# A hybrid gMLP and dilated-attention layer on one core: heads in one pipeline, gating inside the attention, last values through the rows' buffers

## The chip, the cores and the metric

The kernel runs on one core of a Trainium2 chip. A core has TensorE (PE in the profile, its weight loads PEld), VectorE (DVE), ScalarE (ACT), GpSimd (POOL) and SyncE (SP), whose queue issues nearly all DMAs here. The metric is the device time of one execution in microseconds. The kernel before took 1597.32 us, the median of 3 runs (1597.07 to 1600.4).

## The reference

One layer over 1024 tokens of width 1024, in float32:

```python
h = rms_norm(x, g_pre); proj = h @ w_in          # u, v, z_A, q, k, v_B, z_B, gate_A, gate_B
y_a = u' * (W_s LN(v') + b) * silu(z_a)           # gMLP: 16 groups, mixing inside 128-token chunks
for (window, dilation) in ((128,1),(512,4),(2048,16)):
    s = q.k * E**-0.5 - slope*dist                # 8 heads of 128, ALiBi, |j| <= 64 steps
    o, lse = softmax(s) @ v, logsumexp(s)
y_b = sum(softmax(lse over patterns) * o) * silu(z_b)
m = sigmoid(gate_a)*(y_a @ w_pa) + sigmoid(gate_b)*(y_b @ w_pb)
out = x + rms_norm(m @ w_o, g_post)
```

## The kernel before

Every float32 product is made as three products of rounded parts: an operand is split into a high part (ACT copies it into a rounded type) and a low part (the rest, a subtraction on DVE or POOL), and PE adds high by high, high by low and low by high. So each product needs an ACT and a DVE or POOL instruction ahead of PE.

The stages, in order of time:
- **Rows and attention values.** Tiles of x are normalised and transposed; `vb` is the product with the value columns of `w_in`, made in banks for several chunks at once. `v_out` (line 249) splits a bank into `vh` and `vl` and stores both to DRAM. `vh` has two buffers of the tag "ws", `vl` two of its own. The last call of `rows_product` ends with four such banks.
- **Projections.** All other columns of `w_in` go through a seven-product scheme (`seven`, line 369). The first column block is `gates(0)`: its products are called `g0p`. Its second product, `p6`, needs a sum of two weight blocks (`weight_sum`, line 364 in `sum_of`), and that sum's tile has the tag "ws" too. Then come the gMLP columns with the mixing.
- **Attention beside the A projection.** For each head: `scores` (eight pairs of 128-query tiles; half 1 is the residue classes, half 0 the chunks, of which 0 and 7 are the end chunks with narrower windows), the exponentials on ACT, `exchange` of maxima and sums between the two layouts (16 small copies on POOL, 16 on DVE), `normalise`, `scale` of the weights, and `weigh`: nine stages (four residues, chunks 1 and 3, the ends, chunks 5 and 7), each transposing weights on PE (line 723), splitting the transposed bank (`pth`, `ptl`), and multiplying with the values (`pr` line 742, `pc` line 757) two stages later (`LAG`). The sum of both is `o`, stored to `o_d` (line 804). The products of the A projection (`pa`, lines 857 to 859) are cut into 256 steps of three products; `BESIDE` says how many go with each stage, `PAIRS` how many score pairs of the next head. After its ninth stage a head takes its last two stages' products at once, and then the next head begins.
- **Tail.** `gated_heads` loads `o_d` and the gate `z_d` for two heads and half the tokens at a time, multiplies them on POOL (line 925) and splits the result into `yh`, `yl`; the steps that are left run beside it. Then PE makes `pb` (lines 977 to 979), and last the output projection with the final norm.

The order of instructions on each engine is set when the program is built, by a list scheduler over the code's order; the engines then run their own lists in order and wait on semaphores. Buffers of one tag are reused in rotation: who takes one waits until its last reader, a store included, is done.

Of the kernel before, what the change touches and what calls it, by code (L numbers as in the profile page):

```python
# [9 lines left out]
F32 = mybir.dt.float32  # L10
# [26 lines left out]
def tile_hybrid_encoder(  # L37
# [164 lines left out]
    with tc.tile_pool(name="start", bufs=1) as sp:  # L202
# [46 lines left out]
        def v_out(c, cb, ps):  # L249
            vh = wpool.tile([P, 512], F32R, tag="ws", bufs=2, name=f"vh{cb}{c}")  # L250
            vl = sp.tile([P, 512], F32R, tag="vl", bufs=2, name=f"vl{cb}{c}")
            split(vh, vl, ps)
            for t, d in ((vh, v_hi), (vl, v_lo)):
                stored.append(nc.sync.dma_start(d[c * P:(c + 1) * P, 512 * cb:512 * (cb + 1)], f32(t)))
# [321 lines left out]
    with tc.tile_pool(name="heads", bufs=1) as hp, tc.tile_pool(name="attn", bufs=1) as ap:  # L576
# [45 lines left out]
        def scores(h, res):  # L622
# [6 lines left out]
            order = [(1, (i, i + 1)) for i in (0, 2, 4, 6)] + [(0, (0, 7)), (0, (1, 2)), (0, (3, 4)), (0, (5, 6))]  # L629
            for half, pair in order:  # L630
                ps = bank("sc", f"sc{h}{half}{pair[0]}").rearrange("p (t n) -> p t n", t=2)
                st = (hp if half else ap).tile([P, 2, 256], F32, tag=f"st{half}", bufs=8 if half else 6, name=f"st{h}{half}{pair[0]}")
# [79 lines left out]
        def weigh(h, res):  # L712

# [83 lines left out]
            for stage in begun:  # L797
                take(stage)

            for b in range(2):  # L800
                hs = slice(512 * b, 512 * (b + 1))
                o4 = o[:, hs].rearrange("p (a i r) -> p a i r", a=4, r=4)
                nc.vector.tensor_tensor(o4, po[b].rearrange("p (a r i) -> p a i r", a=4, r=4), o4, ALU.add)
                nc.sync.dma_start(o_d[h][:, hs], o[:, hs])

# [14 lines left out]
        PAIRS = (2, 2, 2, 2, 0, 0, 0, 0, 0)  # L820
        BESIDE = (2, 1, 1, 2, 1, 2, 3, 3, 3, 4)
# [62 lines left out]
        for _ in queries_keys(1, heads[1]):  # L884
            take(steps, 3)
        for h in range(H):
# [3 lines left out]
            for i, _ in enumerate(weigh(h, heads[h])):  # L890
                take(pairs, PAIRS[i])
                take(steps, BESIDE[i])
                if i == 3 and more:
                    residue_values(h + 1, heads[h + 1])
                if more and i == 3:
                    take(exchange(h + 1, heads[h + 1], 0))
                    late = exchange(h + 1, heads[h + 1], 1)
                if more and i in (5, 6):
                    take(late, 1)
                if more and i == 7:  # L900
                    normalise(h + 1, heads[h + 1])
                if more and i == 8:
                    for tile_ in TILES[0] + TILES[1]:
                        scale(heads[h + 1], *tile_)
                if i > 4:
                    take(ahead, 1)
            if more:
                chunk_values(h + 1, heads[h + 1])
            take(ahead)
            take(steps, BESIDE[9])  # L910


    with tc.tile_pool(name="tail", bufs=1) as tp:
# [3 lines left out]
        def gated_heads(h, b):  # L917

            bs = slice(512 * b, 512 * (b + 1))
            o, z = [tp.tile([P, 2, 512], F32, tag=t, bufs=n, name=f"{t}{h}{b}") for t, n in (("o", 2), ("z", 1))]  # L920
# [8 lines left out]
        ready = (_ for h in range(0, H, 2) for b in range(2) for _ in gated_heads(h, b))  # L929
# [133 lines left out]
```

## Time and profile before

| what | value |
|---|---|
| median of 3 runs | 1597.32 us |
| the profiled execution, its span | 1596.76 us, 1595.0 us |
| PE busy | 1519.5 us, 95% |
| DVE, POOL, ACT busy | 55%, 48%, 43% |
| mean granted clock of PE | 0.982 |
| DMA | 252.16 MB, 158 GB/s over the span |

PE is busy nearly throughout, so time is to be found where PE stands or runs at the lower clock. A busy matmul is counted from its start to its modelled end and overlaps the next one; the pace of PE is seen in the distance between starts.

### The profile page before, as it was taken

The page shows a single profiled execution, that of the slowest core. Times are in us where ns is not written, and L with a number is a line of the kernel's source. Part 1 is how long each engine was busy: PE and PEld are TensorE (multiplying, and loading weights), DVE is VectorE, ACT ScalarE, POOL GpSimd, SP SyncE. Part 2 cuts the span into 40 slices and gives each one's busy share as a digit, 9 for nine tenths or more (in the row PEclk, how much of TensorE's full clock was granted, in tenths as well). Part 3 has the DMA queues.
Part 4 walks back from the last instruction along what each step waited for, and adds up shares of the span by engine and source line. Part 5 has one row for each costly group of instructions (what it writes and reads, how often), then busy time and mean ns, then how long its engine had stood idle before and what let it go on. Part 6 is the DMA issues. An engine that isn't in the chain of part 4 may idle for free. (4 is left out here: it accounts for less than half of the span.)

```text
span 1595.0 us, 22762 instructions
## 1 busy us (share of the span) xinstructions
PE 1519.5 (95%) x7863; PEld 1277.7 (80%) x7863; DVE 882.6 (55%) x1706; ACT 689.7 (43%) x1315; POOL 769.4 (48%) x703
## 2 busy tenths in 40 slices
PE   8998999999999999999999999989998989979998
PEld 4786999988888888788788888778787767758886
DVE  5723444476675665857564655577777575232112
ACT  5522433343433434343444444677766565221111
POOL 2413544465555555555555555454444443664132
PEclk9999999999999999999999999999999989989999
DMA  8445333334534443636344443586666657785531
GB/s 258 157 166 177 117 103 107 111 126 132 165 122 149 130 154 106 184 101 188 110 146 136 131 138 123 188 234 196 207 186 187 205 161 206 223 248 175 198 106 66
DMA packets 247812, 252.16 MB, mean 158 GB/s; under 512 B 14184, under 2 KB 187272, under 8 KB 247440
## 3 DMA queue, kind: packets, MB, share of 16 engines
q1 hardware_dynamic: 247328, 249.88, 49.9%
q8 instruction: 62, 1.02, 0.3%
q10 hardware_dynamic: 368, 0.82, 0.2%
q14 instruction: 54, 0.44, 0.1%
HBM read 174.10 MB, written 76.55 MB: 157 GB/s over the span
## 5 line engine op out<-in xcount | busy, mean ns | idle before, releaser
L108 POOL TENSOR_TENSOR wl_pa<-wr_pa,wh_pa 128x512 fp32r<-128x512 f32 x56 | 73.7, 1322 | 98.1 <-ACT wh_pa L106 89.5
L512 DVE TENSOR_SCALAR vn<-vn,mean,rstd 128x128 f32<-128x128 f32 x128 | 57.1, 500 | 35.1 <-DMA vn<-v_d 34.8
L665 ACT ACTIVATE st<-st,own 128x256 f32<-128x256 f32 (+1 forms) x128 | 62.9, 492 | 24.7 <-DVE own L661 24.3
L977 PE MATMUL pb<-yh,wh_pb 128*128 128x512 f32 x128 | 50.6, 396 | 10.2 <-ACT yh L159 10.2
L978 PE MATMUL pb<-yl,wh_pb 128*128 128x512 f32 x128 | 50.8, 397 | 1.5 <-DVE yl L160 1.4
L106 ACT ACTIVATE wh_pa<-wr_pa 128x512 fp32r<-128x512 f32 x64 | 38.9, 624 | 28.8 <-PE pa L858 16.0
L678 DVE COPY oth<-own 32x4 f32<-32x4 f32 x128 | 47.3, 369 | 5.6 <-ACT st L665 3.5
L979 PE MATMUL pb<-yh,wl_pb 128*128 128x512 f32 x128 | 50.3, 393 | 0.0
L678 POOL COPY oth<-own 32x4 f32<-32x4 f32 x128 | 27.2, 212 | 38.5 <-ACT st L665 33.5
L981 POOL TENSOR_TENSOR mb<-thb,mb 128x512 f32<-128x512 f32 x16 | 20.6, 1288 | 45.7 <-DVE thb L980 36.2
L1012 ACT ACTIVATE sq<-o 128x512 f32<-128x512 f32 x16 | 9.6, 598 | 74.6 <-PE o L1010 74.6
L160 POOL TENSOR_TENSOR vl<-vn,vh 128x512 fp32r<-128x512 f32 x32 | 41.3, 1290 | 0.8 <-ACT vh L159 0.8
L160 DVE TENSOR_TENSOR yl<-o,yh 128x512 fp32r<-128x512 f32 x16 | 18.2, 1135 | 39.4 <-ACT yh L159 38.7
L992 DVE TENSOR_TENSOR sso<-sso 128x1 f32<-128x1 f32 x8 | 1.3, 159 | 67.6 <-ACT sq L1012 67.6
L160 POOL TENSOR_TENSOR qcl<-q,qch 128x512 fp32r<-128x512 f32 x16 | 25.8, 1621 | 26.0 <-ACT qch L159 26.0
L977 PEld LDWEIGHTS pb<-yh,wh_pb 128*128 128x128 f32 x128 | 24.4, 191 | 16.1 <-ACT yh L159 11.0
L160 DVE TENSOR_TENSOR vl<-vb,vh 128x512 fp32r<-128x512 f32 x16 | 10.9, 688 | 44.0 <-ACT vh L159 36.2
L661 DVE CUSTOM_DVE_ANT_0 st<-sc,tb 128x256 f32<-128x256 f32 x64 | 24.9, 419 | 17.7 <-PE sc L660 10.3
L165 POOL TENSOR_TENSOR sso<-sso,mhalf 128x1 f32<-128x1 f32 x8 | 4.4, 550 | 59.1 <-DVE sso L164 59.1
L658 PE MATMUL sc<-krh,qch 128*128 128x256 f32 (+1 forms) x80 | 24.6, 309 | 8.2 <-DVE own L661 7.6
L108 POOL TENSOR_TENSOR wl_wos<-wr_wos,wh_wos 128x512 fp32r<-128x512 f32 x16 | 20.7, 1294 | 22.8 <-ACT wh_wos L106 22.8
L160 DVE TENSOR_TENSOR ptla<-pa,ptha 128x512 fp32r<-128x512 f32 (+1 forms) x32 | 19.8, 619 | 20.1 <-ACT ptha L159 19.9
(2640 smaller groups left out, 5857.3 us busy)
## 6 DMA issues: line engine op xcount, KB each, us to landing
wr_pa<-in_w_proj_a_dram SPq DMA_DIRECT2D x32, 512.0 KB, 5.1
wr_g<-in_w_in_dram SPq DMA_DIRECT2D x16, 512.0 KB, 3.6
wr_va<-in_w_in_dram SPq DMA_DIRECT2D x16, 512.0 KB, 3.7
wr_u<-in_w_in_dram SPq DMA_DIRECT2D x16, 512.0 KB, 4.4
wr_z<-in_w_in_dram SPq DMA_DIRECT2D x16, 512.0 KB, 4.3
vn<-v_d SPq DMA_DIRECT2D x32, 256.0 KB, 2.8
y_d<-s SPq DMA_DIRECT2D x32, 256.0 KB, 3.0
wr_yf<-y_d SPq DMA_DIRECT2D x16, 512.0 KB, 6.6
```

The source lines that it names most:

```text
L106: nc.scalar.activation(hi, src, AF.Copy)
L108: low.tensor_tensor(lo, src, f32(hi), ALU.subtract)
L160: low.tensor_tensor(lo, src, f32(hi), ALU.subtract)
L512: nc.vector.tensor_scalar(vn[:, c, :], vn[:, c, :], mean[:, 4 * b + c, 0:1], rstd[:, 4 * b + c:4 * b + c + 1], op0=ALU.subtract, op1=ALU.mult)
L658: nc.tensor.matmul(dst, lhs[0], rhs[0], start=True, stop=False)
L661: nc.vector.tensor_tensor_reduce(st[:, t, :n], ps[:, t, :n], bias, -1.0, -NEG, ALU.add, ALU.min, own[:, half, idx, 0:1])
L665: nc.scalar.activation(st[:, t, :n], st[:, t, :n], AF.Exp, bias=own[:, half, idx, 0:1], scale=-1.0, accum_out=own[:, half, idx, 1:2])
L678: (nc.gpsimd, nc.vector)[half].tensor_copy(dst, src)
L977: nc.tensor.matmul(ps, lh, rh, start=(k == 0), stop=False)
L978: nc.tensor.matmul(ps, lh, rl, start=False, stop=False)
L979: nc.tensor.matmul(ps, ll, rh, start=False, stop=(k == KT - 1))
L981: nc.gpsimd.tensor_tensor(ma, th, ma, ALU.add)
```

## The change

Four edits:
- `v_out` writes the values of the second column block (cb = 1) into tiles of the tag "xt" (six buffers that held the rows of x), one tile for high and low, instead of "ws" and "vl".
- `scores` takes the end chunks' pair last; the two `st` tags have 7 buffers each instead of 8 and 6.
- `weigh` no longer finishes its last two stages at once: it yields, and the main loop takes these two from the head before (`before`) in the first rounds of the next head. `PAIRS`, `BESIDE` and the rounds in which `exchange`, `normalise` and `chunk_values` are called change; score pairs are now taken one per step of the A projection.
- `weigh` loads the head's gate (`zt`, tag "ws"), multiplies `o` by it on POOL and stores the gated result; the tail only loads and splits (`load_heads`), the low parts alternating between DVE and POOL, into three tiles in rotation.

```diff
         def v_out(c, cb, ps):
-            vh = wpool.tile([P, 512], F32R, tag="ws", bufs=2, name=f"vh{cb}{c}")
-            vl = sp.tile([P, 512], F32R, tag="vl", bufs=2, name=f"vl{cb}{c}")
+            if cb:
+                vhl = sp.tile([P, 2, 512], F32R, tag="xt", bufs=6, name=f"vhl{c}")
+                vh, vl = vhl[:, 0, :], vhl[:, 1, :]
+            else:
+                vh = wpool.tile([P, 512], F32R, tag="ws", bufs=2, name=f"vh{c}")
+                vl = sp.tile([P, 512], F32R, tag="vl", bufs=2, name=f"vl{c}")
...
-            order = [(1, (i, i + 1)) for i in (0, 2, 4, 6)] + [(0, (0, 7)), (0, (1, 2)), (0, (3, 4)), (0, (5, 6))]
+            order = [(1, (i, i + 1)) for i in (0, 2, 4, 6)] + [(0, (1, 2)), (0, (3, 4)), (0, (5, 6)), (0, (0, 7))]
...
-            for stage in begun:
+            zs = []
+            for b in range(2):
+                zs.append(wpool.tile([P, 512], F32, tag="ws", bufs=2, name=f"zt{h}{b}"))
+                nc.sync.dma_start(zs[b], z_d[h][:, 512 * b:512 * (b + 1)])
+            for i, stage in enumerate(begun):
                 take(stage)
+                if i + 1 < len(begun):
+                    yield
...
+                nc.gpsimd.tensor_tensor(o[:, hs], o[:, hs], zs[b], ALU.mult)
                 nc.sync.dma_start(o_d[h][:, hs], o[:, hs])
+            yield
...
-        PAIRS = (2, 2, 2, 2, 0, 0, 0, 0, 0)
-        BESIDE = (2, 1, 1, 2, 1, 2, 3, 3, 3, 4)
+        PAIRS = (2, 1, 2, 2, 0, 1, 0, 0, 0)
+        BESIDE = (3, 2, 2, 3, 2, 3, 3, 3, 3)
...
-            for i, _ in enumerate(weigh(h, heads[h])):
-                take(pairs, PAIRS[i])
-                take(steps, BESIDE[i])
+            stages = weigh(h, heads[h])
+            for i in range(9):
+                take(stages, 1)
+                take(before, 1)
+                for j in range(BESIDE[i]):
+                    if j < PAIRS[i]:
+                        take(pairs, 1)
+                    take(steps, 1)
...
             take(ahead)
-            take(steps, BESIDE[9])
+            before = stages
+        for _ in before:
+            take(steps, 3)
...
-        def gated_heads(h, b):
...
-            for t, src in ((o, o_d), (z, z_d)):
-                nc.sync.dma_start(t, src[h:h + 2, :, bs].rearrange("k p n -> p k n"))
+        def load_heads(h, b):
+
+            tag, n = (("o", 2), ("z", 1))[h // 2 % 3 == 2]
+            t = tp.tile([P, 2, 512], F32, tag=tag, bufs=n, name=f"yf{h}{b}")
+            nc.sync.dma_start(t, o_d[h:h + 2, :, 512 * b:512 * (b + 1)].rearrange("k p n -> p k n"))
             for i in range(2):
                 y[h + i, b] = [tp.tile([P, 512], F32R, name=f"y{s}{h + i}{b}") for s in "hl"]
-                nc.gpsimd.tensor_tensor(o[:, i, :], o[:, i, :], z[:, i, :], ALU.mult)
-                split(*y[h + i, b], o[:, i, :])
+                split(*y[h + i, b], t[:, i, :], (nc.vector, nc.gpsimd)[i])
```

Three places show what moves. The first is ACT's list where the last value banks are split and the first projection begins; `vh` and `vhl` are high parts of the values, `wh_g0p` high parts of the weights of `g0p` (from a raw block `wr_g`, or from a sum `ws_g0s`), `g0u` the first product's copy. Before:

```order
L106 ACTIVATE wh_g0p_1221<-wr_g_1216 128x512
L159 ACTIVATE vh_1184<-vb_0_1084 128x512
L159 ACTIVATE vh_1190<-vb_1_1085 128x512
L159 ACTIVATE vh_1196<-vb_2_1086 128x512
L159 ACTIVATE vh_1202<-vb_3_1087 128x512
L106 ACTIVATE wh_g0p_1244<-ws_g0s_1242 128x512
L384 ACTIVATE g0u_1237<-g0p_1220 128x512
L106 ACTIVATE wh_g0p_1261<-wr_g_1218 128x512
```

And now:

```order
L106 ACTIVATE wh_g0p_1213<-wr_g_1208 128x512
L106 ACTIVATE wh_g0p_1236<-ws_g0s_1234 128x512
L106 ACTIVATE wh_g0p_1253<-wr_g_1210 128x512
L159 ACTIVATE vhl_1180<-vb_0_1080 128x512
L159 ACTIVATE vhl_1185<-vb_1_1081 128x512
L159 ACTIVATE vhl_1190<-vb_2_1082 128x512
L159 ACTIVATE vhl_1195<-vb_3_1083 128x512
L388 ACTIVATE g0u_1229<-g0p_1212 128x512
```

The weights of the second and third product of `g0p` are rounded ahead of the last four value banks instead of behind them.

The second place is PE where head 2 ends and head 3 begins; `pa` are steps of the A projection, `pb30` transposes the first weights of head 3, `pc21` are products of head 2's last chunks, `sc410` scores of head 4. Before:

```order
L857 MATMUL pa05_11068<-ya0310h_9866,wh_pa0511_10965 128x512
L858 MATMUL pa05_11068<-ya0310l_9867,wh_pa0511_10965 128x512
L859 MATMUL pa05_11068<-ya0310h_9866,wl_pa0511_10967 128x512
L723 MATMUL pb30_11486<-ident_69,st310_11045 128x128
L723 MATMUL pb30_11486<-ident_69,st314_11087 128x128
L723 MATMUL pb30_11486<-ident_69,st310_11045 128x128
L723 MATMUL pb30_11486<-ident_69,st314_11087 128x128
L658 MATMUL sc410_11498<-krh4_11304,qrh4_11300 128x256
L659 MATMUL sc410_11498<-krl4_11305,qrh4_11300 128x256
L660 MATMUL sc410_11498<-krh4_11304,qrl4_11301 128x256
L658 MATMUL sc412_11510<-krh4_11304,qrh4_11300 128x256
```

And now:

```order
L872 MATMUL pa06_11426<-ya0000h_9661,wl_pa0600_10950 128x512
L728 MATMUL pb30_11508<-ident_69,st310_11057 128x128
L728 MATMUL pb30_11508<-ident_69,st314_11110 128x128
L728 MATMUL pb30_11508<-ident_69,st310_11057 128x128
L728 MATMUL pb30_11508<-ident_69,st314_11110 128x128
L762 MATMUL pc21_11360<-ptha25_11399,va02_11006 128x256 x2
L762 MATMUL pc21_11360<-ptha25_11399,va12_11016 128x256 x2
L762 MATMUL pc21_11360<-ptla25_11400,va02_11006 128x256 x2
L662 MATMUL sc410_11530<-krh4_11344,qrh4_11340 128x256
L663 MATMUL sc410_11530<-krl4_11345,qrh4_11340 128x256
L664 MATMUL sc410_11530<-krh4_11344,qrl4_11341 128x256
L870 MATMUL pa06_11426<-ya0111h_9675,wh_pa0601_10987 128x512
```

Head 2's products of chunk 5 stand behind the next head's first transposes now, and the second score pair stands behind a step of the A projection.

The third is DVE at the same place: `st` are weights being scaled, `ptla25` and `ptla27` low parts of head 2's chunks 5 and 7, `o2` its result. Before:

```order
L704 TENSOR_SCALAR st310_11045<-st310_11045,nm3_11382 128x256
L160 TENSOR_TENSOR ptla27_11397<-pa27_11393,ptha27_11396 128x256
L704 TENSOR_SCALAR st314_11087<-st314_11087,nm3_11382 128x256
L704 TENSOR_SCALAR st310_11045<-st310_11045,nm3_11382 128x256
L704 TENSOR_SCALAR st314_11087<-st314_11087,nm3_11382 128x256
L803 TENSOR_TENSOR o2_11031<-pc20_11319,o2_11031 128x512
L863 TENSOR_TENSOR tha04_11287<-tha04_11287,pa04_10927 128x512
```

And now:

```order
L708 TENSOR_SCALAR st310_11057<-st310_11057,nm3_11466 128x256
L708 TENSOR_SCALAR st314_11110<-st314_11110,nm3_11466 128x256
L708 TENSOR_SCALAR st312_11072<-st312_11072,nm3_11466 128x256
L708 TENSOR_SCALAR st316_11155<-st316_11155,nm3_11466 128x256
L708 TENSOR_SCALAR st312_11072<-st312_11072,nm3_11466 128x256
L160 TENSOR_TENSOR ptla25_11400<-pa25_11394,ptha25_11399 128x512
L708 TENSOR_SCALAR st316_11155<-st316_11155,nm3_11466 128x256
L876 TENSOR_TENSOR tha05_11329<-tha05_11329,pa05_10952 128x512
L160 TENSOR_TENSOR ptla27_11443<-pa27_11439,ptha27_11442 128x256
L814 TENSOR_TENSOR o2_11033<-pc20_11359,o2_11033 128x512
```

Seven scalings of head 3 (two more st310 and st314 stand ahead of these rows) now come ahead of the low part of chunk 5 of head 2.

## Rows read from the trace of the kernel before

**Rows 1.** The page, its first part: busy time of each engine.

```profile
PE 1519.5 (95%) x7863; PEld 1277.7 (80%) x7863; DVE 882.6 (55%) x1706; ACT 689.7 (43%) x1315; POOL 769.4 (48%) x703
```

**Rows 2.** Windows by stage: length, busy us and count by engine, clock, DMA.

```profile
core 0: us, PE busy (x) PEld busy (x) DVE busy (x) ACT busy (x) POOL busy (x), PEclk, DMA share, GB/s
...
134.80:163.50 28.70, 22.48 (x87) 17.54 (x86) 15.28 (x17) 12.36 (x22) 17.27 (x12) 0.88 0.79 271
...
1060.00:1357.50 297.50, 270.71 (x1599) 229.83 (x1600) 207.35 (x578) 192.88 (x460) 133.72 (x199) 0.95 0.65 194
1357.50:1425.00 67.50, 52.87 (x219) 41.30 (x219) 23.02 (x23) 19.63 (x33) 45.37 (x33) 0.92 0.78 237
...
1498.60:1584.70 86.10, 86.10 (x379) 70.78 (x378) 13.38 (x30) 10.96 (x31) 20.49 (x21) 1.00 0.27 96
```

**Rows 3.** Timeline, 137 to 150 us: start, length, engine, line, instruction, wait.

```profile
137.55 0.39 PE L412 MATMUL g0p<-hT00h,wl_g0p 128*128 128x512 f32 x1
...
142.44 0.69 DVE L364 TENSOR_TENSOR ws_g0s<-ws_g0s,wr_g 128x512 f32<-128x512 f32 x1 [1.19 <-DMA vb_h<-vh]
143.22 0.63 ACT L106 ACTIVATE wh_g0p<-ws_g0s 128x512 fp32r<-128x512 f32 x1 [3.29 <-DVE ws_g0s L364]
...
143.90 0.79 PE L408 MATMUL g0p<-t2h,wh_g0p 128*128 128x512 f32 x1 [5.97 <-ACT wh_g0p L106]
...
149.81 0.39 PE L408 MATMUL g0p<-hT10h,wh_g0p 128*128 128x512 f32 x1
```

**Rows 4.** Windows, the stretch behind that wait.

```profile
145.00:150.00 5.00, 4.75 (x12) 3.66 (x12) 2.58 (x2) 2.45 (x5) 5.00 (x5) 0.52 0.96 383
```

**Rows 5.** Instructions on the tile vh: its stores, from issue to landing.

```profile
DMA to landing us min/median/max: 2.1/2.7/4.9
```

**Rows 6.** Waits of PE, 1060 to 1357.5 us: total, times, longest.

```profile
PE sc L658 <- DVE own L661: 11.1, 9, 2.6
PE pc L757 <- ACT ptha L159: 5.3, 4, 2.8
PE pc L757 <- DVE ptla L160: 4.3, 4, 2.9
PE pa L723 <- DVE ptle L160: 3.3, 1, 3.3
```

**Rows 7.** Windows of 10 us in the attention with a lower clock.

```profile
1060.00:1070.00 10.00, 9.05 (x32) 7.33 (x33) 7.42 (x12) 8.29 (x16) 7.81 (x7) 0.66 0.60 203
...
1090.00:1100.00 10.00, 8.02 (x29) 6.60 (x30) 7.33 (x26) 4.49 (x11) 4.32 (x4) 0.66 0.70 211
...
1290.00:1300.00 10.00, 7.14 (x21) 5.19 (x21) 9.81 (x24) 3.69 (x10) 5.97 (x6) 0.50 0.43 124
```

**Rows 8.** Timeline of DVE where head 3 ends and head 4 begins.

```profile
1200.59 5.15 DVE L678 COPY oth<-own 32x4 f32<-32x4 f32 x8
...
1208.23 2.52 DVE L704 TENSOR_SCALAR st<-st,nm 128x256 f32<-128x256 f32 x4
```

**Rows 9.** Timeline of POOL, the same stretch.

```profile
1201.07 3.03 POOL L160 TENSOR_TENSOR qcl<-q,qch 128x512 fp32r<-128x512 f32 x2 [2.24 <-ACT qch L159]
```

**Rows 10.** Line L678 (exchange copies): ns min/median/max, first and last start.

```profile
L678 DVE COPY oth<-own x128: 147/161/1561, 1051.9 to 1327.7; 32x4 f32<-32x4 f32 x128
```

**Rows 11.** Line L704 (scaling on DVE).

```profile
L704 DVE TENSOR_SCALAR st<-st,nm x64: 334/388/1411, 1059.2 to 1333.8; 128x256 f32<-128x256 f32 x64
```

**Rows 12.** Waits of PE, 1357.5 to 1425 us.

```profile
PE pb L977 <- ACT yh L159: 10.2, 1, 10.2
PE pa L857 <- DVE tha L863: 3.0, 2, 1.7
```

**Rows 13.** Line L925 (gating in the tail).

```profile
L925 POOL TENSOR_TENSOR o<-o,z x16: 1260/1290/1731, 1369.4 to 1419.5; 128x512 f32<-128x512 f32 x16
```

**Rows 14.** Line L922 (loads of o and z in the tail).

```profile
DMA to landing us min/median/max: 4.7/5.3/6.8
```

**Rows 15.** Line L804 (stores of o).

```profile
DMA to landing us min/median/max: 2.0/2.1/2.3
```

More of the change, by code (lines that the diff above doesn't have):

```diff
@@ L628, in scores @@
             wts = res["wts"] = {}
-            order = [(1, (i, i + 1)) for i in (0, 2, 4, 6)] + [(0, (0, 7)), (0, (1, 2)), (0, (3, 4)), (0, (5, 6))]
+            order = [(1, (i, i + 1)) for i in (0, 2, 4, 6)] + [(0, (1, 2)), (0, (3, 4)), (0, (5, 6)), (0, (0, 7))]
             for half, pair in order:
                 ps = bank("sc", f"sc{h}{half}{pair[0]}").rearrange("p (t n) -> p t n", t=2)
-                st = (hp if half else ap).tile([P, 2, 256], F32, tag=f"st{half}", bufs=8 if half else 6, name=f"st{h}{half}{pair[0]}")
+                st = (hp if half else ap).tile([P, 2, 256], F32, tag=f"st{half}", bufs=7, name=f"st{h}{half}{pair[0]}")
                 n = 256
@@ L885, in tile_hybrid_encoder @@
             take(steps, 3)
+        before = iter(())
         for h in range(H):
@@ L893, in tile_hybrid_encoder @@
                 if i == 3 and more:
                     residue_values(h + 1, heads[h + 1])
-                if more and i == 3:
                     take(exchange(h + 1, heads[h + 1], 0))
                     late = exchange(h + 1, heads[h + 1], 1)
-                if more and i in (5, 6):
+                if more and i in (6, 7):
                     take(late, 1)
-                if more and i == 7:
+                if more and i == 8:
                     normalise(h + 1, heads[h + 1])
-                if more and i == 8:
@@ L903, in tile_hybrid_encoder @@
                     for tile_ in TILES[0] + TILES[1]:
                         scale(heads[h + 1], *tile_)
+                    chunk_values(h + 1, heads[h + 1])
                 if i > 4:
                     take(ahead, 1)
-            if more:
-                chunk_values(h + 1, heads[h + 1])
             take(ahead)
-            take(steps, BESIDE[9])
+            before = stages
+        for _ in before:
+            take(steps, 3)
     with tc.tile_pool(name="tail", bufs=1) as tp:
         y = {}
-        def gated_heads(h, b):
-            bs = slice(512 * b, 512 * (b + 1))
-            o, z = [tp.tile([P, 2, 512], F32, tag=t, bufs=n, name=f"{t}{h}{b}") for t, n in (("o", 2), ("z", 1))]
-            for t, src in ((o, o_d), (z, z_d)):
-                nc.sync.dma_start(t, src[h:h + 2, :, bs].rearrange("k p n -> p k n"))
+        def load_heads(h, b):
+            tag, n = (("o", 2), ("z", 1))[h // 2 % 3 == 2]
+            t = tp.tile([P, 2, 512], F32, tag=tag, bufs=n, name=f"yf{h}{b}")
+            nc.sync.dma_start(t, o_d[h:h + 2, :, 512 * b:512 * (b + 1)].rearrange("k p n -> p k n"))
@@ L923, in gated_heads @@
             for i in range(2):
                 y[h + i, b] = [tp.tile([P, 512], F32R, name=f"y{s}{h + i}{b}") for s in "hl"]
-                nc.gpsimd.tensor_tensor(o[:, i, :], o[:, i, :], z[:, i, :], ALU.mult)
-                split(*y[h + i, b], o[:, i, :])
+                split(*y[h + i, b], t[:, i, :], (nc.vector, nc.gpsimd)[i])
                 yield
-        ready = (_ for h in range(0, H, 2) for b in range(2) for _ in gated_heads(h, b))
+        ready = (_ for h in range(0, H, 2) for b in range(2) for _ in load_heads(h, b))
```

## The prediction

> **What bounds the kernel now.** The page's busy shares come first: PE is busy 95% of the span, no other engine over 55% [rows 1]. That does not say that PE is at its pace, so the windows by stage come next [rows 2]. In the output projection nothing disturbs PE: 379 products in 86.1 us, 0.227 us from one to the next. That is the price of a product of 512 columns, and three make a step of the A projection, 0.68 us. Measured by it, three stretches fall short. The first projection `g0p` stands 6.2 us of its 28.7 and runs at a mean clock of 0.88. The attention from 1060 us on stands 26.8 of 297.5 us at 0.95. The 67.5 us behind it stand 14.6 us at 0.92. A time won elsewhere would lie beside PE's work. So I read three views for these stretches: the timeline around the first gap [rows 3, 4], and PE's waits in the other two [rows 6, 12].
>
> The order of the changed kernel has 7477 rows on PE against 7479, by the way rows are merged: no product goes and none comes. The change can only close gaps or open new ones, and I count it as three terms.
>
> **Term 1, the values through the rows' buffers.** PE issues the last product of the first step of `g0p` at 137.55 and the first of the third step at 149.81 [rows 3]. Between these lie the 12 products of the second step, 2.7 us by 0.227, and one pace of the first, 0.2. So 9.3 us are lost. The timeline says to what: PE waited 6 us for the rounded weights, ACT for the weight sum, DVE for a store of `vh` to land, since sum and `vh` share the two buffers of "ws". The rest is the clock: in the next 5 us PE made 12 products at a granted 0.52 [rows 4], half of full speed and so the 1.2 of the two levels, after it had stood. In the changed order the sums stand ahead of the last values on DVE, and ACT rounds the weights of the second and third step ahead of the four value copies, with no "ws" buffer to wait for. PE goes from the first step into the second, and the drop of the clock goes with the wait before it.
>
> What is late next: the fourth step's weights. Their sum and the copy of the first product lie in a pool that reuses the memory of "xt", so both wait until the last value store has landed. The last four banks are done at about 134; four roundings of 0.63 us and a subtraction of 0.69 (the lengths of the like instructions in rows 3) make the last low part ready at about 137, and its store follows by 137.5, an estimate. With the median landing of 2.7 us [rows 5] they are done at 140.2, with the longest, 4.9, at 142.4. Sum, rounding and low part take 0.69, 0.63 and 1.4 more; PE wants the high part at about 143.2 and the low one half a microsecond later. So the wait is nothing by the median and about 2 us by the maximum. I take -8 us, bounds -4 (a second such delay, from the 2 MB of reloads that queue behind the stores at 383 GB/s) and -9.3.
>
> **Term 2, gating inside the attention.** The tail's z tile has one buffer, so load, multiplication on POOL and split run in a row for each pair of heads: 16 multiplications start between 1369.4 and 1419.5 [rows 13], 6.7 us per pair. PE has 56 steps to run beside it, 38 us, and then stands 10.2 us at the first `pb` for `yh` [rows 12], 14.6 us in all, and some 2 us more go at the half clock behind it: 16.5 us.
>
> Now the tail only loads and splits, with three tiles in rotation. A tile's round is the landing, 5.3 us [rows 14], two roundings of 0.63 and a low part of 1.29, 7.9 us: 2.6 per pair, 21 us for eight pairs. It begins some 3 us after the last attention product (addition 0.7, multiplication 1.29, issue), so the last pair is ready at about 24 us. The order gives PE 33 steps there, 22.4 us, and the seventh pair is only needed 4 us into `pb`. I leave 2 us of waits: -14, bounds -9 (the waits for `tha` remain and the loads slip by 4 us) and -16.5.
>
> In the attention the gate adds per head two loads, two multiplications of 1.29 us on POOL, which is busy 133.7 of 297.5 us [rows 2], and a wait: `o` has one buffer, and ACT's copy of the next head's residues into it now waits for addition, multiplication and a store's landing of 2.1 us [rows 15]. That is 0.7 + 1.3 to 2.6 + 0.4 + 2.1, 4.5 to 6 us. Queued behind that copy are ACT's exponentials and `pth`. But the order puts the first copy directly ahead of the second, behind chunk 3's `ptha`, where PE has done some 11 us of work since the head's last product: covered. Behind POOL's multiplication stand `wl_pa` parts that PE wants about a head later. I cost both at nothing, and at up to 1 us a head if the cover shrinks.
>
> **Term 3, the heads as one pipeline.** The lost time is 26.8 us of standing and, from the three windows below 0.7, (0.34 + 0.34 + 0.50) x 10 = 11.8 us of clock [rows 7]: 39 us at most. The waits [rows 6]: 11.1 us for score banks (PE puts out two pairs in a row, DVE reduces them behind its other work), 9.6 us for `pth` and `ptl` where a head ends, 3.3 for the ends' low part. The new order puts a step between two pairs and moves the additions of `o` behind them; I take half of the 11.1. The head's last products now have the next head's transposes and steps around them, and between the last score of a head and the first transposes that need its scaling stand 11 steps instead of 10, 0.7 us more cover. But `ptla` of chunk 5 now stands behind seven scalings of 0.388 us each by the median [rows 11] instead of ahead of them, and PE asks for it right behind the four transposes: some 1.5 us new at each of seven boundaries. So of the 12.9 for the splits little goes, 2 us net, and of the clock 3.5. Together -11. Bounds: -30 (nearly all goes), and +10 (the new wait as long as the longest seen there, 3.3 us, at seven boundaries, less what the scores give).
>
> **The sum.** -8 - 14 - 11 = -33 us on the profiled execution's 1596.8 us (its span of 1595.0 and 1.8 around it), which is 0.5 us under the median of the runs: 1564 us.
>
> **A rule that speaks against it.** While POOL ran two strided subtractions for 3.03 us [rows 9], eight copies of DVE, 0.161 us each by the median, took 5.15 us [rows 8, 10]. The Trainium skill, SBUF — State Buffer, section "SBUF: two separate sides", says why: DVE and GpSimd share a port pair by an exclusive lock, and whoever comes second stands until the other's instruction ends. By that rule the trace agrees, and each moved multiplication may stop DVE.
>
> **Rivals.**
> - *Only the two ends pay.* The new wait behind the scalings eats what the spread scores give. For it: the best heads in the trace already lose little, and half the loss lies in three spots that a new order need not spare. 1596.8 - 22 = 1575 us. Chance 0.25.
> - *DVE stops at each boundary; slower.* PE makes the four transposes and stands until five more scalings and `ptla` are done. With scalings at up to 1.4 us [rows 11] that is up to 7.7 us, and a window at 0.66 behind such a wait costs 3.4 us more [rows 7]. At 4 + 3.4 us on seven boundaries it is +52, less the 22: 1627. It decides from 3.2 us per boundary on. Against it: the 11 steps ahead let DVE get in front. Chance 0.10.
> - *The gate stops DVE.* POOL's 14 multiplications in the loop hold DVE's scalings and copies for 1.29 us each: +18 us, 1582. Against it: when they run, DVE mostly reads PSUM, and those lengths hardly vary. The shared port of the page named above would be the cause. Chance 0.07.
> - *Nearly all gaps close.* 1596.8 - 9 - 16 - 30 = 1541. Chance 0.08.
>
> **How the numbers follow.** The forecast has 0.50, with 1553 to 1572 as its own range. A difference of 0.2% (3 us) is about what a measurement can tell from none. Slower by more than that is the second rival, 0.10; within it, the tail of the first and the third, 0.03; faster 0.87. The range of 1540 to 1592 takes in term 3's bounds together with the ends' smallest gains, and leaves out the slow rival.
>
> **What would show it.** Right: the third step of `g0p` begins within 2 us of 141, and no clock below 1 there; the first `pb` waits under 3 us for `yh`; PE stands under 20 us between the first and the last head, with a wait of `pc` for `ptla` behind the first transposes of each head. Wrong: `g0p` waits for a store, `pb` waits 10 us, or PE's waits in the heads grow past 27 us.

## The result, and the profile after

The changed kernel takes 1578.07 us, the median of four runs (1574.23 to 1580.57), against 1597.19 of the kernel before in the same measurement: a ratio of 0.9875, 95% interval 0.9848 to 0.9902, some 20 us faster where 33 were forecast. The time lies in the range of 1540 to 1592, but above the 1553 to 1572 of the likeliest case. It is nearest to the first rival's 1575, "only the two ends pay".

The profiled execution took 1580.57 us, the slowest of the four. The page's first part answers [rows 1]:

```profile
PE 1519.4 (96%) x7863; PEld 1280.5 (81%) x7863; DVE 862.8 (55%) x1698; ACT 688.2 (44%) x1315; POOL 778.6 (49%) x711
```

PE's work is the same 1519 us, so what is gained are gaps. The windows by stage answer [rows 2] (the first projection, the heads, the steps behind them with the first columns of `pb`):

```profile
core 0: us, PE busy (x) PEld busy (x) DVE busy (x) ACT busy (x) POOL busy (x), PEclk, DMA share, GB/s
134.80:159.90 25.10, 22.28 (x85) 17.81 (x85) 11.04 (x15) 9.32 (x16) 9.66 (x7) 0.86 0.81 288
1059.00:1371.50 312.50, 287.05 (x1667) 243.78 (x1667) 202.38 (x579) 194.83 (x466) 160.12 (x219) 0.94 0.70 204
1371.50:1430.00 58.50, 56.34 (x247) 45.78 (x245) 16.59 (x23) 20.64 (x36) 38.02 (x29) 1.00 0.80 254
```

The stretch behind the heads has its clock back, 1.00 for 0.92, and PE stands 2 us there. In the heads it stands 25.5 us and the clock is 0.94: before it was 26.8 us and 0.95. Here and in the first projection the forecast gain is missing.

**Term 1's place.** The timeline around the first gap answers [rows 3]; PE now goes from the first step into the second without a stop, as forecast, and stops behind it:

```profile
140.07 0.39 PE L416 MATMUL g0p<-t2h,wl_g0p 128*128 128x512 f32 x1
142.62 0.60 ACT L388 ACTIVATE g0u<-g0p 128x512 f32<-128x512 f32 x1 [6.97 <-DMA vb_l<-vhl]
142.68 0.69 DVE L368 TENSOR_TENSOR ws_g0s<-wr_g 128x512 f32<-128x512 f32 x1 [6.30 <-DMA vb_l<-vhl]
143.27 0.79 PE L412 MATMUL g0p<-hT10h,wh_g0p 128*128 128x512 f32 x1 [2.82 <-ACT g0u L388]
```

The third step begins at 143.27, not at 141. The row says why: it waits for the copy `g0u` of the first product, and that copy for the last value store. In `seven`, `p2` is added into `p1`'s bank (`into`), so the bank must have been read first. The clock behind this stop answers [rows 4]; columns are length, PE busy, clock, DMA share, GB/s:

```profile
143.00:150.00 7.00, 6.73 (x17) 0.54 0.77 314
```

In this execution a stop of 2.8 us was followed by as long a stretch at half clock as the one of 6.0 us before, some 6.8 us, counted from its beginning inside the stop. Other executions with the like stop had a shorter one or none (below, with the values alone), so this row does not show what such a stop costs in general.

**Term 2's place.** PE's waits from 1371.5 to 1430 us answer [rows 12]:

```profile
PE pb L993 <- ACT yh L159: 1.7, 1, 1.7
PE pb L994 <- DVE yl L160: 0.2, 1, 0.2
PE pb L994 <- POOL yl L160: 0.2, 1, 0.2
```

10.2 us have become 1.7, and the waits for `tha` are gone.

**Term 3's place.** PE's waits in the heads, 1059 to 1371.5 us, answer [rows 6]:

```profile
PE pb L728 <- DVE ptla L160: 11.5, 4, 6.6
PE sc L662 <- DVE own L665: 7.0, 6, 3.3
PE pb L728 <- DVE st L708: 4.6, 2, 4.2
PE pa L871 <- DVE ya1310l L160: 2.1, 2, 1.8
PE pe L728 <- DVE ptla L160: 2.0, 1, 2.0
```

Score banks cost 7.0 us for 11.1. Of the 12.9 us for splits (9.6 where a head ends, 3.3 inside a head) 2.6 are left, all inside a head: 2.0 at `pe` and 0.6 at `pa`, which is below these rows. But 11.5 us stand in a place that had none: at the next head's transposes, for the low part of the last head's chunk. They are 6.6 us at one boundary and 0.9 to 2.0 at three; at the other three PE does not stop for `ptla`. Of the 4.6 us for `st`, 4.2 stand ahead of the first head and end before this window begins; the kernel before stood 3.3 us there. The timeline of DVE and POOL at the longest of these stops (head 3 to head 4; PE stood from 1211.5 to 1218.07) answers [rows 8, 9]:

```profile
1208.96 2.72 POOL L706 TENSOR_SCALAR st<-st,nm 128x256 f32<-128x256 f32 x2 [4.07 <-DVE nm L700]
1209.16 1.09 DVE L160 TENSOR_TENSOR qrl<-q,qrh 128x512 fp32r<-128x512 f32 x1
1210.17 5.72 DVE L708 TENSOR_SCALAR st<-st,nm 128x256 f32<-128x256 f32 x7
...
1211.65 1.55 POOL L160 TENSOR_TENSOR qcl<-q,qch 128x512 fp32r<-128x512 f32 x1
...
1213.15 2.58 POOL L108 TENSOR_TENSOR wl_pa<-wr_pa,wh_pa 128x512 fp32r<-128x512 f32 x2
...
1215.70 1.31 POOL L160 TENSOR_TENSOR ya1111l<-wr_yf,ya1111h 128x512 fp32r<-128x512 f32 x1
1215.81 0.68 DVE L160 TENSOR_TENSOR ptla<-pa,ptha 128x512 fp32r<-128x512 f32 x1
1216.41 0.67 DVE L876 TENSOR_TENSOR tha<-tha,pa 128x512 f32<-128x512 f32 x1
1217.01 0.68 DVE L160 TENSOR_TENSOR ya1111l<-wr_yf,ya1111h 128x512 fp32r<-128x512 f32 x1
1217.61 0.41 DVE L160 TENSOR_TENSOR ptla<-pa,ptha 128x256 fp32r<-128x256 f32 x1
```

Seven scalings took 5.72 us, 0.82 each and not the 0.388 that I had counted, while POOL worked without a break. And PE's transposes begin right when the low part of chunk 7 (the 128x256 row, done at 1218.02) has left its bank.

To compare stages over all runs I take three lengths from the starts of instructions: **P**, from the first product of `g0p` to the heads' first transposes; **A**, from there to the last product `pc`, less 0.68 us for each step of the A projection in it (176 before, 199 with the pipeline); **T**, from that product to the last of `pb`, less the steps likewise (56 and 33). Before: P 924.6, A 176.8, T 105.1. After: 923.8, 176.6, 90.0. So term 1 brought 0.8 us here, term 2 15.1 and term 3 next to nothing. For A I also give what the half clock costs in it: the part of full speed that was not granted, added up over windows of 1 us. That is 13.7 us before and 18.2 after.

### The profile page after: what moved, and what is told of

The parts are those of the page before. It is cut to its first block, busy times and chain, and to the rows that moved or that the text cites. A ratio compares the mean times of both kernels' runs of the same rounds, so it can differ in the third digit from the quotient of the medians.

```text
span 1578.8 us, 22737 instructions
## 1 busy us (share of the span) xinstructions
PE 1519.4 (96%) x7863; PEld 1280.5 (81%) x7863; DVE 862.8 (55%) x1698; ACT 688.2 (44%) x1315; POOL 778.6 (49%) x711
## 4 chain that ended last, share of the span: by engine, by line
PE 72%; DVE 8%; issue 5%; ACT 4%; DMA 4%; POOL 3%; SPq 1%; DVEq 0%; ACTq 0%; POOLq 0%
PE pa L870 2%; PE pa L871 2%; PE pb L994 2%; PE pb L995 2%; PE pb L993 2%; PE pa L872 2%; PE sg L527 2%; PE vb L154 1%; PE vb L156 1%; PE vb L155 1%; ACT st L669 1%; POOL out L1014 1%; PE pr L747 1%; DMA vn<-v_d 1%; DVE vn L516 1%
## 5 line engine op out<-in xcount | busy, mean ns | idle before, releaser
L665 DVE CUSTOM_DVE_ANT_0 st<-sc,tb 128x256 f32<-128x256 f32 x64 | 25.5, 421 | 28.9 <-PE sc L664 23.6
L682 DVE COPY oth<-own 32x4 f32<-32x4 f32 x128 | 34.3, 268 | 12.3 <-ACT st L669 10.6
L160 POOL TENSOR_TENSOR qcl<-q,qch 128x512 fp32r<-128x512 f32 x16 | 27.9, 1756 | 26.3 <-ACT qch L159 26.3
L728 PE MATMUL pb<-ident,st 128*128 128x128 f32 x128 | 23.3, 294 | 16.2 <-DVE ptla L160 11.5
L815 POOL TENSOR_TENSOR o<-o,zt 128x512 f32<-128x512 f32 x16 | 20.6, 1295 | 36.2 <-DMA zt<-z_d 18.0
L682 POOL COPY oth<-own 32x4 f32<-32x4 f32 x128 | 23.9, 187 | 24.3 <-ACT st L669 19.4
L728 PEld LDWEIGHTS pb<-ident,st 128*128 128x128 f32 x128 | 16.7, 150 | 21.9 <-DVE ptla L160 13.2
L160 DVE TENSOR_TENSOR ptlb<-pb,pthb 128x512 fp32r<-128x512 f32 x32 | 21.9, 688 | 16.3 <-ACT pthb L159 16.1
L108 POOL TENSOR_TENSOR wl_vb<-wr_vb,wh_vb 128x512 fp32r<-128x512 f32 x14 | 18.2, 1310 | 25.0 <-ACT wh_vb L106 25.0
```

Of the source, the lines that this page charges most:

```text
L108: low.tensor_tensor(lo, src, f32(hi), ALU.subtract)
L160: low.tensor_tensor(lo, src, f32(hi), ALU.subtract)
L682: (nc.gpsimd, nc.vector)[half].tensor_copy(dst, src)
L728: nc.tensor.transpose(pt[:n, c0:c0 + P], src, ident)
```

## The experiments

Every ratio is against the kernel before, run on the same chip between the others. Its medians there are 1596.6 to 1596.9 us, so times of different experiments can be compared.

**The values alone (t1_alone).** The kernel before with the new `v_out`.

> The kernel before with the one edit in v_out (last values through the rows' buffers). Theory A (the term was mis-sized): the second step of g0p joins the first, but its sum lies in the bank of p1, so the third step, which adds to that bank, waits for the copy g0u, and that copy for a value store; the third step begins at about 143.3 instead of 149.8, yet the half clock follows all the same, so the end comes only 3 to 4 us earlier: 1594 against 1597. Rival B (the term is as forecast and something else ate it in the full change): 8 us, 1589.

1591.61 us, 0.9969 (0.9957 to 0.9981): 5.0 us gained, between the two. The third step began at 142.66 and waited 2.40 us for `g0u`; P is 919.4. Theory A has the wait right, but not the clock: behind this stop PE ran at full clock. Columns as in the window above:

```profile
143.00:150.00 7.00, 7.00 (x32) 1.00 0.90 326
```

Eight of the profiles have this stop, of 2.4 to 3.0 us. Behind it the half clock lasted 6.8 us in one (the changed kernel's first), 3.4 us in three, and did not come in four; stops of 2.8 us stand in the first group and in the last. What decides it no run shows.

**No pipeline (no_pipe).** The changed kernel with the old loop (and with its score order, buffers, `PAIRS` and `BESIDE`):

```diff
-            for i in range(9):
-                take(stages, 1)
-                take(before, 1)
-                for j in range(BESIDE[i]):
-                    if j < PAIRS[i]:
-                        take(pairs, 1)
-                    take(steps, 1)
+            for i in range(9):
+                take(stages, 1)
+                take(pairs, PAIRS[i])
+                take(steps, BESIDE[i])
...
+            take(stages)
```

> The changed kernel with the head loop, the score order and the buffers of before: values and gating edits stay, the pipeline across heads goes. Theory A (the pipeline gains nothing: waits behind the scalings and a longer half clock eat what the spread scores give): 1578, within 3 us of the changed kernel; the waits for score banks come back at about 11 us and the waits for ptla at pb go. Rival B (the pipeline is worth its forecast 11 us in most runs, and the one profile of it is an outlier): 1585 or more. Rival C (it costs): 1573 or less.

1585.77 us, 0.9931 (0.9919 to 0.9943), so theory A, that the pipeline gains nothing, falls, and by the number rival B holds: taking the pipeline out costs 9.4 us against the changed kernel beside it (1576.41). But P, A, T are 918.6, 187.1, 87.0, where the values alone have A 177.1: gating inside the old loop makes the heads 10 us *longer*, which the tail's 18 us pay for. Two views show how. The first is the wait of ACT's queue ahead of the copies of `o`, which has one buffer that the store still reads (ns min/median/max):

```profile
L750 ACTq EVENT_SEMAPHORE  x14: 17/158/4344, 1110.4 to 1345.7; - x14
```

ACT stood 4.3 us at the longest; in the changed kernel, and in the kernel before, none of these waits exceeds 0.04 us. The second is the timeline of DVE and POOL at a head's end, where DVE's scalings and a subtraction stretch while POOL gates:

```profile
1252.96 2.62 DVE L708 TENSOR_SCALAR st<-st,nm 128x256 f32<-128x256 f32 x2
...
1254.13 2.57 POOL L815 TENSOR_TENSOR o<-o,zt 128x512 f32<-128x512 f32 x2
...
1255.50 1.74 DVE L160 TENSOR_TENSOR ya1201l<-wr_yf,ya1201h 128x512 fp32r<-128x512 f32 x1
```

So what the pipeline does is to cover the cost of the gate, which I had put at nothing, covered by "some 11 us of work": that cover is the pipeline's. The changed kernel's two profiles show it: none of the gate's 16 multiplications runs beside a scaling of DVE. Beside nearly all of them DVE reads PSUM or does nothing, and its lengths are the undisturbed ones (0.68 us for a `ptlb`, 0.41 for a score reduction).

**Tiles of their own for the first projection (g0_own).** `g0u` and the sum of the fourth step leave the memory of the rows' buffers:

```diff
+            if name == "g0u20":
+                return wpool.tile([P, 512], F32, tag="th", bufs=2, name=name)
-                    pool, tag = early if n in ("s1", "s2") else (ap, "s")
+                    pool, tag = early if n in ("s1", "s2") else (wpool, "th") if (name, n) == ("g0", "s3") else (ap, "s")
```

> The changed kernel with two tiles of the first projection (the copy g0u and the sum of its fourth step) in buffers that do not lie over the rows' buffers. Theory A (the copy's wait for the value stores holds the third step, and the stop brings the half clock): the third step begins at about 140.5, no clock below 1 near there, 6 us gained: 1572 against 1578. Rival B (the half clock comes anyway): the wait of 2.8 us goes, 2 to 3 us gained: 1575. Rival C (another value store or the reloads hold the step): nothing gained.

1572.79 us, 0.9848 (0.9832 to 0.9863), 3.6 us under the changed kernel beside it. The windows of 2 us over the same place show no stop and a full clock, and P is 915.5, some 5 us under the changed kernel's next profile (below). Theory A holds: the copy's wait held the step, and without it there is neither stop nor half clock. P is 915.5 to 916.6 in the three profiles with this edit (two of them further down) and 918.6 to 923.8 in the eight that have the stop. (The two ratios' intervals just touch; that the stop is gone is certain, the 3.6 us less so.) Columns as in the window above:

```profile
142.00:144.00 2.00, 2.00 (x11) 1.00 0.98 369
144.00:146.00 2.00, 2.00 (x11) 1.00 1.00 422
146.00:148.00 2.00, 2.00 (x10) 1.00 0.83 283
148.00:150.00 2.00, 2.00 (x10) 1.00 0.90 278
```

**The changed kernel again (after_again).**

> The changed kernel once more, for its scatter of 1574 to 1581 us. Theory A: the median stays at 1578 and a profile near 1575 differs from the first one in the attention only, by fewer or shorter half-clock stretches there. Rival B: the scatter comes from the loads at the start or from the first projection, and the attention is equal.

1576.41 us (1574.5 to 1578.75), 0.9875 (0.9862 to 0.9887). This profile, of 1576.30 us, has P 920.3, A 172.9, T 91.1. It stops at the same boundaries, with the same 11.5 us for `ptla`; the two profiles differ by 3.8 us in the heads and 3.5 in P, so both theories hold a part. In the heads PE stands 24.3 us for 25.5, and the half clock costs 15.4 us for 18.2: behind the same stops two of its stretches are shorter, 4.0 us for 7.0 and 7.0 for 10.5. The one in the first projection is 3.4 us for 6.8. It sets term 3 at 0 to 4 us.

**Fewer scalings on DVE (scale_act).**

```diff
-            elif half:
+            elif half and idx % 4 < 2:
                 nc.vector.tensor_scalar(w, w, f, None, op0=ALU.mult)
```

> The changed kernel with four of the eight residue scalings per head moved from DVE to ACT, so that four instead of seven scalings stand ahead of the low part of chunk 5 on DVE. Theory A (DVE's list at the end of a head bounds the boundary: the wait of the next head's transposes for ptla, 13.5 us over the heads): three scalings of 0.4 to 0.8 us less at each boundary, the wait falls to 6 us or less, 1569 to 1571 against 1576. Rival B (what is late there is ACT or POOL, or the wait only changes its name): within 2 us of 1576, with waits for the high parts ptha or pthb instead.

1584.81 us, 0.991 (0.9894 to 0.9927): 6 us *slower* than the changed kernel by the ratios, 8 by the medians, which neither side expected. The longest stop fell to 4.4 us, but stops of 2.1 to 3.4 us came at boundaries that had had 0 to 2, and the wait of `pb` for `ptla` grew from 11.5 to 14.7 us (the 13.5 of the expectation takes in the 2.0 at `pe`, inside a head). PE stands 26.3 us in the heads, little more than the 24.3 and 25.5 of the changed kernel, but the half clock costs 25.5 us. The timeline at one of the stops:

```profile
1177.08 2.44 ACT L710 ACTIVATE st<-st,nm 128x256 f32<-128x256 f32 x6
...
1180.34 0.36 ACT L159 ACTIVATE ptha<-pa 128x256 fp32r<-128x256 f32 x1
...
1180.73 0.42 DVE L160 TENSOR_TENSOR ptla<-pa,ptha 128x256 fp32r<-128x256 f32 x1 [2.24 <-ACT ptha L159]
...
1181.21 1.11 PE L728 MATMUL pb<-ident,st 128*128 128x128 f32 x4 [3.44 <-DVE ptla L160]
```

Six scalings on ACT now stand ahead of the high part of chunk 7, DVE stands 2.24 us for it, and PE for DVE. The wait names DVE and is ACT's: rival B by its cause, though its number, no change, is wrong too.

**Pairs together (pairs_together).**

```diff
-                for j in range(BESIDE[i]):
-                    if j < PAIRS[i]:
-                        take(pairs, 1)
-                    take(steps, 1)
+                take(pairs, PAIRS[i])
+                take(steps, BESIDE[i])
```

> The changed kernel with the score pairs of a round taken together again, ahead of the round's steps, everything else of the pipeline kept. Theory A (one step between two pairs is what took the waits for score banks from 11 to 5 or 7 us): they come back to 10 us or more, 1580 to 1582 against 1576. Rival B (they fell for another reason, the additions of o behind the first rounds): the waits stay at 5 to 7 us and the time within 2 us of 1576.

1576.17 us, 0.9864 (0.9849 to 0.988), with 5.8 us of waits for score banks: no difference, rival B. The step between two pairs, on which I had built the half of term 3 that came true, is not what shortened these waits.

**Weights' low parts on DVE (wl_dve).**

```diff
-                                      nc.vector if (b, p) == (0, 0) else nc.gpsimd)
+                                      nc.vector)
```

> The changed kernel with the low parts of the A projection's weights on DVE instead of POOL: 53 subtractions of 1.31 us leave POOL, DVE takes as many of about 0.69, 36 us more on an engine that is busy 56%. Theory A (POOL's instructions on SBUF hold up DVE's): DVE's scalings and small copies return to their undisturbed lengths (scalings from 0.47 to under 0.40 us on average), the wait for ptla falls, and the time is the same or up to 8 us shorter, 1568 to 1576. Rival B (DVE's lengths have nothing to do with POOL): the scalings stay at 0.47 us, DVE's list is longer everywhere, and the time grows by 5 to 15 us.

1570.49 us, 0.9828 (0.9814 to 0.9843), 6 us under the changed kernel: theory A. DVE takes 0.78 us for each of its new subtractions, some 41 us *more* work, and yet its busy time in the heads grows by 18 us only (202.2 to 219.9): its small copies take 0.215 us on average for 0.280, the scalings 0.433 for 0.48 (not under 0.40: POOL still has its own scalings and `qcl` at that place). The wait of `pb` for `ptla` hardly fell, from 11.5 to 10.8 us; in all PE stands 21.7 us in the heads for 24.3, and the half clock costs 11.9 for 15.4. The rival that POOL's shorter list did it finds nothing in the changed kernel's trace: no wait of DVE in the heads is put down to POOL, and of PE under 0.5 us.

**The price alone (port).** No layer, only DVE and POOL in phases that both begin together (it leaves out the whole computation).

> A kernel that leaves out the whole layer and writes zeros and ones: the disputed price alone. 24 scalings on DVE (128x256 in SBUF) alone, beside 12 plain POOL subtractions (128x512 in SBUF), and beside 12 strided ones; 16 subtractions on DVE that read PSUM, alone and beside POOL; 40 copies of 32x4 alone and beside POOL; POOL alone. Theory A (POOL holds up DVE where both work on SBUF): a scaling takes 0.39 us or less alone and about a POOL instruction longer, 1.2 to 1.7 us, beside POOL; the copies likewise, 0.06 alone and over 1 beside; the subtractions from PSUM keep their 0.69. Rival B (the long scalings in the heads have another cause): the same lengths in all phases, within 10%.

DVE's timeline: 24 scalings alone, beside plain and beside strided POOL subtractions; 16 subtractions from PSUM alone and beside POOL; 40 copies alone and beside POOL:

```profile
4.22 9.27 DVE L81 TENSOR_SCALAR scale<-scale,f 128x256 f32<-128x256 f32 x24
...
14.17 21.15 DVE L81 TENSOR_SCALAR scale<-scale,f 128x256 f32<-128x256 f32 x24
...
36.73 31.08 DVE L81 TENSOR_SCALAR scale<-scale,f 128x256 f32<-128x256 f32 x24
...
68.88 11.57 DVE L83 TENSOR_TENSOR sub<-ps,sub 128x512 f32<-128x512 f32 x16
...
81.25 11.57 DVE L83 TENSOR_TENSOR sub<-ps,sub 128x512 f32<-128x512 f32 x16
...
96.83 7.63 DVE L86 COPY copy<-copy 32x4 f32<-32x4 f32 x40
...
105.01 17.80 DVE L86 COPY copy<-copy 32x4 f32<-32x4 f32 x40
```

POOL's timeline: plain and strided subtractions beside the scalings, plain ones beside DVE's work on PSUM, then plain and strided ones alone:

```profile
15.68 16.00 POOL L94 TENSOR_TENSOR wl<-q,wl 128x512 f32<-128x512 f32 x12
...
37.62 26.16 POOL L97 TENSOR_TENSOR qcl<-q,qcl 128x512 f32<-128x512 f32 x12
...
82.65 13.34 POOL L94 TENSOR_TENSOR wl<-q,wl 128x512 f32<-128x512 f32 x10
...
125.00 10.64 POOL L94 TENSOR_TENSOR wl<-q,wl 128x512 f32<-128x512 f32 x8
...
137.86 17.41 POOL L97 TENSOR_TENSOR qcl<-q,qcl 128x512 f32<-128x512 f32 x8
```

A scaling takes 0.39 us alone. Beside 13 POOL instructions (one more of the same size opens the phase) 24 of them take 11.9 us longer, 0.9 for each POOL instruction, and 21.8 us longer beside the strided ones, 1.7 each. The subtractions that read PSUM take 0.72 us either way. POOL pays nothing: 1.33 and 2.18 us in company and alone. Theory A, with smaller prices than expected (a scaling takes 0.88 and 1.29 us on average in company, not 1.2 to 1.7; a copy 0.19 alone and 0.45 in company, not 0.06 and over 1), and with a direction that I had not expected: of these instructions only DVE's wait.

That is not so for every instruction. The changed kernel's trace has POOL behind DVE where DVE subtracts two operands that both lie in SBUF:

```profile
157.20 1.29 POOL L108 TENSOR_TENSOR wl_va0p<-wr_va,wh_va0p 128x512 fp32r<-128x512 f32 x1 [6.06 <-PE g0p L414]
158.45 1.73 POOL L108 TENSOR_TENSOR wl_va0p<-ws_va00s,wh_va0p 128x512 fp32r<-128x512 f32 x1
...
158.01 1.03 DVE L368 TENSOR_TENSOR ws_va01s<-wr_va,wr_va 128x512 f32<-128x512 f32 x1
```

The second begins 0.6 us before DVE's ends at 159.04, and takes 0.44 us more than the first. The phases of `port` have no such subtraction.

**The turn of the banks kept (turn_kept).** A head has nine stages, and the turn between the bank "tp" and the banks "sc" began anew with each: ninth and first stage both took "tp".

```diff
+        turn = ["tp", "sc"]
+
         def weigh(h, res):
...
-            pr, turn = {}, ["tp", "sc"]
+            pr = {}
```

> The changed kernel with one line moved: the turn between the banks tp (one buffer) and sc goes on from head to head. With nine stages a head and a turn that begins anew, the ninth stage of a head and the first of the next both take tp, so the next head's transposes wait until the low part of chunk 7 has been read out of it. Theory C (that bank is the boundary's wait, not the low part of chunk 5 that the products want): the waits of pb for ptla, 11.5 and 2.0 us, fall to 5 or less, since the low part of chunk 5 is ready 1.5 to 3 us before that of chunk 7; what is left stands at the products of chunk 5 after 1208; 1566 to 1570 against 1576. Theory A (DVE's list ahead of chunk 5 bounds): the wait moves to the products of chunk 5 (pc for ptla) with its full size, within 2 us of 1576.

1574.65 us, 0.987 (0.9847 to 0.9893), no measurable change: theory C has the bank right and the time wrong.

```profile
PE sc L662 <- DVE own L665: 11.2, 10, 2.6
PE pb L730 <- DVE st L708: 5.6, 2, 4.3
PE pb L730 <- DVE ptla L160: 4.4, 1, 4.4
```

The stops of `pb` for `ptla` went from 11.5 to 4.4 us (the 2.0 us of the expectation are those at `pe`); the waits for score banks, next in DVE's list, came back from 5.0 to 7.0 us to 11.2. In the heads PE stands 26.5 us in all, no less than the 24.3 and 25.5 of the changed kernel. So which instruction PE stands at is a matter of banks; that it stands is DVE's lateness. Theory A, with the wait at the scores instead of the products. The half clock costs only 7.8 us here, but this profile is of the fastest of four runs (1570.33 us), and the median does not show that gain.

**Three and four edits together.** `three` is turn, own tiles and weights on DVE; `four` adds the low parts of the query copies:

```diff
-                      t.rearrange("p (a i r) -> p a r i", a=4, r=4), nc.gpsimd)
+                      t.rearrange("p (a i r) -> p a r i", a=4, r=4))
```

> The changed kernel with three edits that shorten it or should: the turn kept across heads, the first projection's two tiles in buffers of their own (4 us measured alone), the weights' low parts on DVE (6 us measured alone). Theory C: the three act at different places and nearly add up, 1556 to 1561. Rival (the turn and DVE's freed list remove the same wait): 1563 to 1566, 10 us below the changed kernel.

> The kernel with three edits, and the low parts of the strided query copies (qcl) on DVE too: POOL's longest instruction on SBUF, 1.5 to 2.2 us, twice a head, goes, and DVE takes 16 strided subtractions of about 1.1 us more. If what POOL still holds up DVE for counts at the heads' ends: 2 to 4 us less than with three edits. Rival (DVE's own 2.2 us a head stand in the same list ahead of the scalings): the same or up to 4 us more.

1566.46 us, 0.9813 (0.9792 to 0.9834), and 1563.46 us, 0.9792 (0.9777 to 0.9808). For `three` the number is the rival's, but its reason is not shown: alone the three edits measured 2 (within the noise), 4 and 6 us, which come to 11 us added up, where 10 were measured. Theory C failed because it gave the turn a gain that it did not have. `four` is 3 us lower, by its medians as expected, but the intervals overlap. It is the fastest version seen: 33 us under the kernel before, with A at 165.3.

**The same edit in the kernel before (before_wl).**

> The kernel before with the low parts of the A projection's weights on DVE instead of POOL, the edit that took 6 us from the changed kernel. Theory A (POOL holds up DVE in the old loop as well, whose scalings took 0.52 us on average, and PE waits there for DVE too): 4 to 6 us less than before, 1591 to 1593. Theory D (only the pipeline made the heads' ends hang on DVE's list, the old loop covers it): within 2 us of 1597. Rival B (DVE's longer list costs here): 1600 or more.

1587.96 us, 0.9943 (0.9926 to 0.9961): 9 us from the old kernel by one word, more than theory A's 4 to 6; A falls from 176.8 to 169.0, with 21.4 us of standing in the heads for 26.8. So POOL's hold on DVE was a price of the heads all along, and the new order neither made nor removed it.

## Why the prediction was right and wrong

- **Term 1, -8: measured -5.0 alone** (0.8 and 4.3 us in P in the two profiles of the changed kernel). The order and the freed buffer did what was said. The step that failed is the one on what is late next. I let the copy of the first product concern the fourth step only, and overlooked that the third adds into the same bank. That the last store landed at 142.6, where I had 142.4, is luck: I took the longest landing, 4.9 us, from an issue at 137.5, and in the trace SP issues it at 138.9 and no store of these tiles takes over 3.1. "The drop of the clock goes with the wait" held only in part: the half clock came back whole in one profile, half as long in the next and not at all in the run alone.
- **Term 2, -14: right.** T is 105.1 before and 90.0 and 91.1 in the two profiles, 14.0 to 15.1 us less; the first `pb` waits 1.7 us, and I had left 2. The cost of nothing in the heads holds with the pipeline, where the gate meets no scaling; in the old loop gating costs 10 us there.
- **Term 3, -11: measured 0 to -4**, the step that makes most of the difference. Score waits gave 4 to 6 us, near the 5.5 counted, though not for the reason given. The splits were to give 2 us net, 12.9 gone and some 10.5 new. In the two profiles 2.6 and 3.9 us of the old waits stayed and 11.5 came new, so they cost 1.2 to 2.5. That 11.5 is near the seven times 1.5 is luck: it is one stop of 6.6 us, where a scaling behind POOL took 0.82 us and not the median's 0.388, three of 0.9 to 2.0, and three boundaries without. I had that hold in [rows 8, 9] and used it for the gate alone. I also looked for the stop at the products of chunk 5; it stands one instruction earlier, at the transposes, for the bank of chunk 7. So PE's standing fell by 1.3 to 2.5 us where 7.5 were forecast. And the clock was to give 3.5 us, in the belief that it comes back with the old stops: the new ones have half clock behind them as well, six stretches for four, and it cost 18.2 and 15.4 us where it had cost 13.7. This is the part of the term that is furthest off.
- The bound of +10 does not come out of its own words: 3.3 us at seven boundaries, less the 5.5 of the scores, is 17.6. And the 3.3 us were measured inside a head, not at a boundary, where the longest wait was 2.9.
- **The rivals.** The first described it: the scalings eat what the scores give, and the ends pay; it leaves out the clock. The second had the right cause, up to 6.6 us at one boundary, but three of the seven stop for 0.9 to 2.0 us and three not for it at all. The third, the gate that stops DVE, is shown for the old loop; in the new one the gate runs beside DVE's work on PSUM, which is the reason that I had given against it.
- The marks set for right and wrong: the third step at 141 and full clock, wrong; `pb` under 3 us, right; PE under 20 us in the heads, wrong at 25.5, the stop ahead of the first head not counted; a wait of `pc` for `ptla`, wrong by one instruction.

What stays open: why the same stop is followed by a longer stretch at half clock in one execution than in another, and why score waits fell without the step between pairs. The first of these is much of the changed kernel's spread: in the slower profile three stretches last 3 to 3.5 us longer, at a cost of about 1.7 us each, and the two profiles are 4.3 us apart.

## What to carry to other kernels

Price an instruction at the place where it will stand, with the neighbours that it will have there: a median over the whole kernel hides what another engine does to it. When a wait is removed, ask for every reader of the bank and buffer that the next instruction writes, accumulations included. An engine that is the busier one may still be the right place for work, when the idle one takes its memory port away. Price the clock behind a stop from several profiles: the same stop was followed by half clock in some executions and not in others.

## What the runs showed of the hardware

Where both worked on SBUF, POOL delayed DVE: scalings of 128x256 lost 0.9 us per plain POOL subtraction of 128x512 and 1.7 us per strided one, and subtractions that read PSUM took 0.72 us either way. POOL lost nothing to these, but stood 0.44 us behind a DVE subtraction of two operands in SBUF. The Trainium skill, SBUF — State Buffer, section "SBUF: two separate sides", tells of the exclusive lock, by which whoever starts first holds the port pair; the trace agrees for both engines.

A stop of PE of 2.8 us was followed by as long a stretch at the 1.2 GHz level, some 6.8 us, as one of 6.0 us in one execution, and in another by none (granted clock 1.00). So what a shortened stop gives back of the clock cannot be read from one profile; in the three profiles without the stop no half clock came at that place.
